# A hybrid decoder layer in split fp32: seven blocks through Strassen's products where five were, and the gates' silu in one ScalarE instruction

## The chip, the cores and the metric

The kernel runs as one program on one core of a Trainium2 chip. The metric is the device time of an execution in microseconds, the median of three runs. The engines are TensorE (PE; its weight loads are PEld), VectorE (DVE), ScalarE (ACT), GpSimd (POOL) and SyncE (SP), which issues most DMAs.

## What is computed

One layer with two token mixers on 256 tokens of width 2048, fp32, then a SwiGLU FFN:

```
u = rmsnorm(x)
[qkv_A | z_A | b_A | a_A | q_B | k_B | v_B | g_B | gate_A | gate_B] = u @ w_in
o_A = rmsnorm(gated_delta_rule(silu(conv(qkv_A)), ...)) * silu(z_A)
o_B = group_norm(retention(rotary(q_B), rotary(k_B), v_B))  * silu(g_B)
h   = x + (sigmoid(gate_A) * o_A + sigmoid(gate_B) * o_B) @ w_out
h   = h + (silu(rmsnorm(h) @ w_gate) * (rmsnorm(h) @ w_up)) @ w_down
out = rmsnorm(h)
```

There are 8 heads in each mixer, with values of width 256.

## The kernel before

Every large product is done in split precision: a weight tile `raw` (128 x 2048) comes by DMA, ScalarE rounds it to `hi` (line 169), VectorE makes `lo = raw - hi` (line 170), and TensorE multiplies the activations, split in the same way, with `hi` and `lo`. There are two `hi`, two `lo` and three `raw` buffers, so that the next tiles are split while TensorE works on one.

Work is a list of *units*, each with one weight tile. In the first phase four blocks of two heads follow each other. A block has 12 feature-major units (keys, queries, values for mixer A with the short convolution, and the rotary parts of mixer B; lines 239 and 244), and five token-major blocks of 512 columns, numbered i = 0 to 4: the values of mixer B, silu gate and sigmoid gate of mixer B, silu gate and sigmoid gate of mixer A.

A plain token-major block is four units of 24 products of 512 columns (lines 296, 297, 301). A block in `SBLK` goes through `strassen` instead: the 2 x 2 form with seven products, in eight units of 21 products of 256 columns (line 372). Its weights come as 512 KB pieces, VectorE first makes four more combinations of each (lines 187 to 189), and the sums of the activations that it needs (`ush`, `usl`) are made once, from the 14th unit on. Its results stay in four PSUM banks until a last copy (line 386) and four VectorE additions (lines 388 to 392) make the tile `Z`.

The eight units of a Strassen block are spread between the block's main units by `SPOS`: (7, 7) means from main unit 7 on, over 7 main units. A block that isn't in `SBLK` stands in the main list. `EARLY` says from which unit on the main products leave the four PSUM banks that Strassen's results need.

Gates are applied in `gate_evac`: ScalarE takes sigmoid of the scaled PSUM (line 881); for silu VectorE then multiplies by the scaled PSUM again (line 883); VectorE multiplies into the mixer's output (line 885), and after the last gate adds the two mixers (line 887). `merge` transposes the sum on TensorE (line 906) and splits it into the operand of the output projection (lines 914, 915). The second half of that operand shares memory with `ush`, so it can be written only after the last Strassen product: block 2's merge waits in a tile `wait` in the buffer of `Z` and is split by `split_rest` (lines 541, 542). Only for the last block the merge follows at once, and the 16 units of the output projection (`wo`) come next.

A scheduler reorders each engine's instructions in this list when the kernel is built; the resulting order is fixed. A second part of the list (the output projection and the FFN) is not touched.

Of the kernel before, what the change touches and what calls it, by code (L numbers as in the profile page):

```python
# [9 lines left out]
AF = mybir.ActivationFunctionType  # L10
ALU = mybir.AluOpType

P = 128
D = 2048
KT = D // P
S = 256
# [6 lines left out]

NWARM = 10
HOLD, SUMS_AT = 2, 14
EARLY = 28
Q2 = 2
SQ = 4
W_AT0, W_AT, W_TR0, W_TR = 6, 1, 5, 1
# [1 line left out]
SP_BEFORE, SP_AFTER = 2, 1  # L31


SBLK = [(), (2, 3), (2, 3), (3,)]
SPOS = [(), ((7, 7), (16, 8)), ((6, 9), (15, 9)), ((10, 14),)]
SIDE = [(b, i) for b in range(NBLK) for i in SBLK[b]]
MAIN = [(b, i) for b in range(NBLK) for i in range(5) if i not in SBLK[b]]

# [28 lines left out]
def kernel(  # L67
# [5 lines left out]
    V, A_, PE, G = nc.vector, nc.scalar, nc.tensor, nc.gpsimd  # L73
# [16 lines left out]
    def ps_turn(who, pools, name):  # L90
        turns_of[who] += 1
        tag, pool = pools[turns_of[who] % len(pools)]
        return pool.tile([P, 512], F32, tag=tag, name=name)
# [4 lines left out]
    def ps_mix(name):  # L98
        if first[0] and unit[0] < EARLY:
            return ps_turn("mix", [("mx", mx), ("pp", pp)], name)  # L100
        return ps_turn("mix", [("mx", mx), ("sp", sp)] if sums_away() else [("mx", mx)], name)

    def ps_unit(name):
        if not first[0]:
            return ps_turn("unit", [("pp", pp), ("mx", mx)], name)
        if unit[0] < EARLY:
            return ps_turn("unit", [("sp", sp)], name)
# [83 lines left out]
    def after(n, fn):  # L191

        events.setdefault(done[0] + n, []).append(fn)
# [88 lines left out]
    def flat(t):  # L282
        return t.rearrange("p a b -> p (a b)")
# [175 lines left out]
    mm = {}  # L459
# [8 lines left out]
    def t2(name):  # L468
        return mixp.tile([P, 512], F32, tag="t2", name=name, bufs=T2B)

    def mt(shape, tag, name, dt=F32):
        return mixp.tile(shape, dt, tag=tag, name=name)

    rstd_t = mixp.tile([P, NC], F32, name="rstd_t")
    rstd_b = mixp.tile([P, S], F32, name="rstd_b")
    Ei = mixp.tile([P, NBLK, 4, P], F32, name="Ei")
# [8 lines left out]
    def halves(t):  # L485
        return t.rearrange("p (a b) -> p a b", a=2)
# [39 lines left out]
    def new_parts(i):  # L526

        mm[i] = act.tile([P, KT // 2, 2, S], F32R, tag=f"a{2 + i}", name=f"m{i}")

    def merged_parts(b, j):  # L530
        k = 4 * (b % 2) + 2 * j
        return mm[b // 2][:, k:k + 2, 0], mm[b // 2][:, k:k + 2, 1]
# [28 lines left out]
    def block(b):  # L561
# [302 lines left out]
        def gate_evac(i, which, silu):  # L864
            def evac(pst):
                if which + "_done" not in T:
                    after(1, lambda: evac(pst))
                    return
                left[0] -= 1
                if left[0] == 0 and b == NBLK - 1:  # L870
                    with tc.high_priority(offset=100):
                        run(pst)
                else:
                    run(pst)

            def run(pst):
                o = T[which]
                for c in range(NC):
                    sg = halves(t2(f"gs_{b}_{i}_{c}"))
                    oc = halves(o[:, c])  # L880
                    A_.activation(sg, pst[c], AF.Sigmoid, scale=rstd_t[:, c:c + 1])
                    if silu:
                        V.scalar_tensor_tensor(out=sg, in0=pst[c], scalar=rstd_t[:, c:c + 1], in1=sg,
                                               op0=ALU.mult, op1=ALU.mult)
                    V.tensor_tensor(out=oc, in0=oc, in1=sg, op=ALU.mult)
                    if left[0] == 0:
                        mm["last"] = V.tensor_tensor(out=halves(T["oa"][:, c]), in0=halves(T["oa"][:, c]),
                                                     in1=halves(T["ob"][:, c]), op=ALU.add).ins
                if left[0] == 0:
                    if b == NBLK - 1:  # L890
                        merge(0)
                        merge(1)
                    else:
                        after(1, lambda: merge(0))
                        after(1, lambda: merge(1))
            return evac

        def merge(j):
            oa = T["oa"]
            if b == 0 and j == 0:  # L900
                new_parts(0)
            ps = ps_mix(f"pmt_{b}_{j}")
            for i in range(2):
                for c in range(NC):
                    f = (2 * j + i) * P
                    PE.transpose(out=ps[:, i * S + c * P:i * S + (c + 1) * P], in_=oa[:, c, f:f + P],
                                 identity=ident)
            if b // 2 not in mm:
                if j == 0:
                    mm["wait"] = flat(mt([P, 5, S], "Z", "wait"))  # L910
                A_.activation(mm["wait"][:, 512 * j:512 * j + 512], ps, AF.Copy)
                return
            hv, lv = merged_parts(b, j)
            A_.activation(hv, halves(ps), AF.Copy)
            V.tensor_tensor(out=lv, in0=halves(ps), in1=hv.bitcast(F32), op=ALU.subtract)
# [15 lines left out]
        for i, evac in enumerate(evacs):  # L931
            if i in SBLK[b]:
                sides.append(strassen(wsm[SIDE.index((b, i))], (uh, ul, LateSums(), usl), z_tiles, f"t{i}" + n,
# [15 lines left out]
    for b in range(NBLK):  # L949
        main, sides = block(b)  # L950
        for i, side in enumerate(sides):
            streams.append((len(mains) + SPOS[b][i][0], SPOS[b][i][1], side))
        mains += main
# [112 lines left out]
    with tc.tile_pool(name="ffn", bufs=1) as ffn:  # L1066
# [200 lines left out]
        with tc.manual_schedule(engines={nc.vector.engine}):  # L1267
# [4 lines left out]
            for c in range(NC):  # L1272
                for q in range(4):
                    ps = ps_sums(f"po_{c}_{q}")
                    for j in range(4):
# [3 lines left out]
                                    in1=wfs[:, 4 * q:4 * q + 4].unsqueeze(2).to_broadcast([P, 4, P]), op=ALU.mult)  # L1279
# [101 lines left out]
```

## Time and profile before

| | us |
|---|---|
| median of 3 runs | 1645.02 (1644.33 to 1645.72) |
| profiled execution | 1644.22 |
| its span | 1642.4 |
| TensorE busy | 1617.0 (98%) |
| VectorE busy | 1304.3 (79%) |
| ScalarE busy | 845.6 (51%) |
| GpSimd busy | 34.6 (2%) |

The times on the page are those of one execution under the profiler; the span goes from its first to its last recorded instruction. Busy shares are means over stages with different limits: what a stage waits for is read from stretches and from the engines in order of time. Matmuls are pipelined: the busy time of one (0.4 us for 512 columns) is longer than the distance to the next, so units are measured from start to start.

### The profile page before, as it was taken

Reading aid. Unit: us, or ns where it says so; the run is one execution under the profiler, and the core shown is the slowest. Engines: PE = TensorE matmul, PEld = TensorE weight load, DVE = VectorE, ACT = ScalarE, POOL = GpSimd, SP = SyncE. Lnnn points to the kernel's source line nnn. Section 1 sums busy time; section 2 is a strip of 40 time slices with the busy share of each in tenths; the row PEclk is TensorE's granted clock in tenths of the full one; section 3 lists DMA queues with packets and bytes.
Section 4 is the critical chain, followed back from the end, with each engine's and each line's share of the span. In section 5 each row is a group of like instructions: output and inputs, shape, how many; then the busy total and the mean of one; then the engine's idle time right before and its main releaser. Section 6 shows DMA issues by size and latency. Waiting matters only on the chain.

```text
span 1642.4 us, 24810 instructions
## 1 busy us (share of the span) xinstructions
PE 1617.0 (98%) x10202; PEld 1406.1 (86%) x10202; DVE 1304.3 (79%) x1680; ACT 845.6 (51%) x873; POOL 34.6 (2%) x64
## 2 busy tenths in 40 slices
PE   8999999999999999999999999999999999999998
PEld 6887888888888888888788888888888888888887
DVE  7797468887898878876776878889988899878764
ACT  5864455455554555445555654444554445545442
POOL 0000000000000000000000100000000000000000
PEclk8999999999999999999999999999999999999999
DMA  7454454555545565444674556556674566755751
GB/s 273 154 179 170 164 176 148 180 167 183 193 156 179 170 201 197 143 166 156 219 268 156 176 181 217 165 167 194 204 244 136 185 193 188 239 180 181 233 197 52
DMA packets 90450, 300.98 MB, mean 183 GB/s; under 512 B 6752, under 2 KB 11104, under 8 KB 74592
## 3 DMA queue, kind: packets, MB, share of 16 engines
q1 hardware_dynamic: 88896, 295.31, 53.8%
q10 hardware_dynamic: 1440, 4.08, 0.7%
q8 instruction: 80, 1.31, 0.3%
q14 instruction: 34, 0.28, 0.0%
HBM read 297.27 MB, written 2.10 MB: 182 GB/s over the span
## 4 chain that ended last, share of the span: by engine, by line
PE 91%; DVE 3%; DMA 1%; ACT 1%; issue 0%; POOL 0%; ACTq 0%; DVEq 0%
PE ps_wd L325 14%; PE pst_su L372 7%; PE ps_t L296 7%; PE ps_t L297 7%; PE ps_t L301 7%; PE ps_wu L325 7%; PE pst_t L372 6%; PE ps_wg L325 6%; PE pst_sg L372 6%; PE ps_r L239 4%; PE ps_wo L239 4%; PE ps_v L239 3%; PE ps_wo L244 2%; PE ps_r L244 2%; PE ps_v L244 1%; PE ps_q L239 1%
## 5 line engine op out<-in xcount | busy, mean ns | idle before, releaser
L169 ACT ACTIVATE hi_t<-raw_t 128x2048 fp32r<-128x2048 f32 (+1 forms) x100 | 183.1, 1831 | 220.8 <-PE ps_t L297 138.8
L170 DVE TENSOR_TENSOR lo_t<-raw_t,hi_t 128x2048 fp32r<-128x2048 f32 (+1 forms) x100 | 218.1, 2181 | 67.9 <-ACT hi_t L169 56.5
L296 PE MATMUL ps_t<-hi_t,u 128*128 128x512 f32 x480 | 192.0, 400 | 0.4 <-ACT vr L827 0.4
L297 PE MATMUL ps_t<-hi_t,u 128*128 128x512 f32 x480 | 188.3, 392 | 0.0
L325 PE MATMUL ps_wd<-hi_wd,f 128*128 128x512 f32 x704 | 170.8, 391 | 1.0 <-DVE f L1191 1.0
L325 PEld LDWEIGHTS ps_wd<-hi_wd,f 128*128 128x128 f32 x704 | 129.9, 188 | 27.4 <-DVE f L1191 1.2
L169 ACT ACTIVATE hi_sg<-raw_sg 128x1792 fp32r<-128x1792 f32 x48 | 81.6, 1702 | 118.7 <-DVE raw_sg L189 68.0
L169 ACT ACTIVATE hi_su<-raw_su 128x1792 fp32r<-128x1792 f32 x48 | 81.5, 1699 | 86.5 <-DVE raw_su L189 51.2
L170 DVE TENSOR_TENSOR lo_su<-raw_su,hi_su 128x1792 fp32r<-128x1792 f32 x48 | 97.0, 2022 | 35.0 <-ACT hi_su L169 19.7
L301 PE MATMUL ps_t<-lo_t,u 128*128 128x512 f32 x480 | 121.6, 392 | 0.0
L169 ACT ACTIVATE hi_wd<-raw_wd 128x2048 fp32r<-128x2048 f32 x44 | 84.3, 1915 | 70.2 <-PE ps_wd L325 27.8
L170 DVE TENSOR_TENSOR lo_wd<-raw_wd,hi_wd 128x2048 fp32r<-128x2048 f32 x44 | 100.6, 2286 | 19.8 <-ACT hi_wd L169 19.7
L170 DVE TENSOR_TENSOR lo_sg<-raw_sg,hi_sg 128x1792 fp32r<-128x1792 f32 x48 | 96.9, 2020 | 16.0 <-PE ps_wd L325 7.8
L296 PEld LDWEIGHTS ps_t<-hi_t,u 128*128 128x128 f32 x480 | 90.2, 188 | 18.7 <-ACT vr L827 0.6
L301 PEld LDWEIGHTS ps_t<-lo_t,u 128*128 128x128 f32 x480 | 89.7, 188 | 18.7
L297 PEld LDWEIGHTS ps_t<-hi_t,u 128*128 128x128 f32 x480 | 90.2, 188 | 17.7
L325 PE MATMUL ps_wd<-lo_wd,f 128*128 128x512 f32 x352 | 89.9, 396 | 3.6 <-DVE lo_wd L170 3.6
L325 PEld LDWEIGHTS ps_wd<-lo_wd,f 128*128 128x128 f32 x352 | 65.6, 190 | 17.2 <-DVE lo_wd L170 4.2
L325 PE MATMUL ps_wg<-hi_wg,h 128*128 128x512 f32 x320 | 78.9, 392 | 0.3 <-ACT hi_wg L169 0.3
L325 PE MATMUL ps_wu<-hi_wu,h 128*128 128x512 f32 x320 | 76.5, 390 | 0.0
L325 PEld LDWEIGHTS ps_wu<-hi_wu,h 128*128 128x128 f32 x320 | 59.2, 188 | 11.7
L325 PEld LDWEIGHTS ps_wg<-hi_wg,h 128*128 128x128 f32 x320 | 58.3, 188 | 11.6 <-ACT hi_wg L169 0.8
(333 smaller groups left out, 3358.5 us busy)
## 6 DMA issues: line engine op xcount, KB each, us to landing
raw_t<-in_wtm_dram SPq DMA_DIRECT2D x60, 1024.0 KB, 4.8
raw_wd<-in_wdown_dram SPq DMA_DIRECT2D x44, 1024.0 KB, 5.2
raw_sg<-in_wst_dram SPq DMA_DIRECT2D x48, 512.0 KB, 3.5
raw_su<-in_wst_dram SPq DMA_DIRECT2D x48, 512.0 KB, 3.6
raw_t<-in_wsm_dram SPq DMA_DIRECT2D x40, 512.0 KB, 3.5
raw_wg<-in_wgate_dram SPq DMA_DIRECT2D x20, 1024.0 KB, 5.1
raw_wu<-in_wup_dram SPq DMA_DIRECT2D x20, 1024.0 KB, 5.2
raw_v<-in_wqk_dram SPq DMA_DIRECT2D x16, 1024.0 KB, 4.8
```

The source lines that it names most:

```text
L169: ia = A_.activation(hi[:, r], w[:, r], AF.Copy)
L170: iv = V.tensor_tensor(out=lo[:, r], in0=w[:, r], in1=hi[:, r].bitcast(F32), op=ALU.subtract)
L239: PE.matmul(o[0], w, flat(a(k)), start=(k == 0), stop=(k == nk - 1), skip_group_check=True)
L244: PE.matmul(o[0][:, :S], lo[:, k * P:(k + 1) * P], a(k)[:, 0], start=False, stop=(k == nk - 1), skip_group_check=joined)
L296: PE.matmul(pst[c], uh[:, k, c * P:(c + 1) * P], w, start=(k == 0), stop=False)
L297: PE.matmul(pst[c], ul[:, k, c * P:(c + 1) * P], w, start=False, stop=False)
L301: PE.matmul(pst[c], uh[:, k, c * P:(c + 1) * P], lo[:, j * 512:(j + 1) * 512], start=False, stop=(k == KT - 1))
L325: PE.matmul(pst[c], u[:, k, c * P:(c + 1) * P], w[:, k], start=(start and k == 0 and q == 0), stop=(stop and k == 3))
L372: PE.matmul(T[bank][:, half * S:(half + 1) * S], op(j), w[:, slot * 256:(slot + 1) * 256], start=(j == 0 and w is hi and h and half == 0), ...
```

## The change

Two blocks more go through Strassen's products: i = 3 (mixer A's silu gate) in block 0, and i = 2 (mixer B's sigmoid gate) in block 3. Their plain units leave the main lists, and the side units are placed anew: in block 0 over nine main units from the 22nd on, so that they reach into block 1; in block 3 over main units 4 to 12 and 13 to 23, where 23 is the block's last main unit. `EARLY` goes from 28 to 20. `wait` moves from the buffer of `Z` to the first half of `Ei`, which only blocks 0 and 1 read. Silu is one ScalarE instruction.

```diff
-EARLY = 28
+EARLY = 20
...
-SBLK = [(), (2, 3), (2, 3), (3,)]
-SPOS = [(), ((7, 7), (16, 8)), ((6, 9), (15, 9)), ((10, 14),)]
+SBLK = [(3,), (2, 3), (2, 3), (2, 3)]
+SPOS = [((22, 9),), ((7, 7), (16, 8)), ((6, 9), (15, 9)), ((4, 9), (13, 11))]
...
-                    A_.activation(sg, pst[c], AF.Sigmoid, scale=rstd_t[:, c:c + 1])
-                    if silu:
-                        V.scalar_tensor_tensor(out=sg, in0=pst[c], scalar=rstd_t[:, c:c + 1], in1=sg,
-                                               op0=ALU.mult, op1=ALU.mult)
+                    A_.activation(sg, pst[c], AF.Silu if silu else AF.Sigmoid, scale=rstd_t[:, c:c + 1])
                     V.tensor_tensor(out=oc, in0=oc, in1=sg, op=ALU.mult)
...
-                    mm["wait"] = flat(mt([P, 5, S], "Z", "wait"))
+                    mm["wait"] = Ei[:, 0:2].rearrange("p a b c -> p (a b c)")
```

TensorE at the end of the first phase, before. `ps_t43` is the last plain block (i = 4 of block 3), `ps_wo1` and `ps_wo0` are the first blocks of the output projection, `m0` and `m1` its operand's halves, `pmt` the last merge's transposes.

```order
L301 MATMUL ps_t43_1_7489<-lo_t43_3_7545,u2_93 128x512 x4
L239 MATMUL ps_wo1_7701<-m0_2039,hi_wo1_7646 128x512 [waits Activation_49]
L239 MATMUL ps_wo1_7701<-m0_2039,hi_wo1_7646 128x512 x7
L239 MATMUL ps_wo1_7701<-m1_7462,hi_wo1_7646 128x512 x4
L906 MATMUL pmt_3_0_7604<-cs_74,oa_3_7121 128x128 [waits DVE_49]
L906 MATMUL pmt_3_1_7611<-cs_74,oa_3_7121 128x128
L239 MATMUL ps_wo0_7658<-m0_2039,hi_wo0_7640 128x512 x8
L239 MATMUL ps_wo0_7658<-m1_7462,hi_wo0_7640 128x512 x4
```

The same place in the changed kernel. `pst_t33` are the results of the Strassen block i = 3 of block 3.

```order
L372 MATMUL pst_t33_1_7183<-lo_t33_7_7771,ush_1103 128x256
L239 MATMUL ps_wo1_7942<-m0_2366,hi_wo1_7887 128x512 [waits Activation_49]
L239 MATMUL ps_wo1_7942<-m0_2366,hi_wo1_7887 128x512 x7
L239 MATMUL ps_wo1_7942<-m1_7825,hi_wo1_7887 128x512 [waits DVE_49]
L239 MATMUL ps_wo1_7942<-m1_7825,hi_wo1_7887 128x512
L239 MATMUL ps_wo1_7942<-m1_7825,hi_wo1_7887 128x512 [waits DVE_49]
L239 MATMUL ps_wo1_7942<-m1_7825,hi_wo1_7887 128x512
L903 MATMUL pmt_3_0_7845<-cs_74,oa_3_7464 128x128 [waits DVE_49,PE_49]
L903 MATMUL pmt_3_1_7852<-cs_74,oa_3_7464 128x128
L239 MATMUL ps_wo0_7899<-m0_2366,hi_wo0_7881 128x512 x8
L239 MATMUL ps_wo0_7899<-m1_7825,hi_wo0_7881 128x512 x4
```

A Strassen product is now the last of the phase, and the products with `m1` wait for VectorE.

ScalarE at that place, before. `hi_wo0` and `hi_wo1` are the splits of the first output weights, `gs_3_2` and `gs_3_3` the gates i = 3 and i = 4 of block 3.

```order
L169 ACTIVATE hi_t43_3_7544<-raw_t43_3_7514 128x2048 [waits DMAHW5_49,DVE_49,PE_49]
L881 ACTIVATE gs_3_2_0_7474<-Z_t33_7467,rstd_t_99 128x512 [waits DVE_49]
L881 ACTIVATE gs_3_2_1_7478<-Z_t33_7467,rstd_t_99 128x512
L169 ACTIVATE hi_wo0_7640<-raw_wo0_7638 128x2048 [waits DMAHW6_49,PE_49,Activation_49]
L169 ACTIVATE hi_wo1_7646<-raw_wo1_7644 128x2048 [waits DMAHW7_49,DVE_49,PE_49]
L881 ACTIVATE gs_3_3_0_7596<-ps_t43_0_7488,rstd_t_99 128x512 [waits DVE_49,PE_49]
L881 ACTIVATE gs_3_3_1_7600<-ps_t43_1_7489,rstd_t_99 128x512 [waits DVE_49,PE_49]
```

The same place in the changed kernel; `s1_t33` is the copy of line 386, `m1<-Ei` the split of block 2's merge.

```order
L169 ACTIVATE hi_wo0_7881<-raw_wo0_7879 128x2048 [waits DMAHW6_49,PE_49,Activation_49]
L881 ACT_TABLE_LOAD
L881 ACTIVATE gs_3_3_0_7798<-ps_t43_0_7581,rstd_t_99 128x512 [waits PE_49]
L881 ACTIVATE gs_3_3_1_7801<-ps_t43_1_7582,rstd_t_99 128x512 [waits PE_49]
L169 ACTIVATE hi_wo1_7887<-raw_wo1_7885 128x2048 [waits DMAHW7_49,DVE_49,PE_49]
L386 ACTIVATE s1_t33_7831<-pst_t33_2_7184 128x256 [waits PE_49,Pool_49]
L541 ACTIVATE m1_7825<-Ei_101 128x2x256 [waits PE_49]
L541 ACTIVATE m1_7825<-Ei_101 128x2x256
L881 ACT_TABLE_LOAD [waits DVE_49]
L881 ACTIVATE gs_3_2_0_7837<-Z_t33_7830,rstd_t_99 128x512 [waits Activation_49]
L881 ACTIVATE gs_3_2_1_7841<-Z_t33_7830,rstd_t_99 128x512 [waits Activation_49]
```

The gate i = 4 has come ahead of the second output weights' split, the gate i = 3 behind it, each with a table load; the second load stands behind a wait for VectorE.

VectorE there in the changed kernel, from the first addition of `Z` to the sum of the mixers:

```order
L388 TENSOR_TENSOR Z_t33_7830<-pst_t33_0_7182,s1_t33_7831 128x512
L542 TENSOR_TENSOR m1_7825<-Ei_101,m1_7825 128x2x256 x2
L389 TENSOR_TENSOR Z_t33_7830<-pst_t33_2_7184,Z_t33_7830 128x256
L390 TENSOR_TENSOR Z_t33_7830<-pst_t33_3_7185,Z_t33_7830 128x512
L392 TENSOR_TENSOR Z_t33_7830<-pst_t33_1_7183,Z_t33_7830 128x512
L882 TENSOR_TENSOR oa_3_7464<-oa_3_7464,gs_3_2_0_7837 128x512
L882 TENSOR_TENSOR oa_3_7464<-oa_3_7464,gs_3_2_1_7841 128x512
L884 TENSOR_TENSOR oa_3_7464<-oa_3_7464,ob_3_7324 128x512 x2
```

The same work before: the additions stood before the subtraction of the last plain unit, and that block's gate came last.

```order
L388 TENSOR_TENSOR Z_t33_7467<-pst_t33_0_6650,s1_t33_7468 128x512
L389 TENSOR_TENSOR Z_t33_7467<-pst_t33_2_6652,Z_t33_7467 128x256
L390 TENSOR_TENSOR Z_t33_7467<-pst_t33_3_6653,Z_t33_7467 128x512
L392 TENSOR_TENSOR Z_t33_7467<-pst_t33_1_6651,Z_t33_7467 128x512
L170 TENSOR_TENSOR lo_t43_3_7545<-raw_t43_3_7514,hi_t43_3_7544 128x2048
```

On VectorE the order now has four additions, two subtractions, two multiplies and two adds in one chain ahead of the merge.

## Rows read from the trace of the kernel before

**Rows 1.** The page, busy time of each engine over the span.
```profile
PE 1617.0 (98%) x10202; PEld 1406.1 (86%) x10202; DVE 1304.3 (79%) x1680; ACT 845.6 (51%) x873; POOL 34.6 (2%) x64
```

**Rows 2.** Stretches: us, busy us (instructions) by engine, granted clock, DMA share, GB/s.
```profile
242.00:270.00 28.00, 28.00 (x168) 24.86 (x167) 25.07 (x51) 15.76 (x36) 1.31 (x5) 1.00 0.36 117
270.00:320.00 50.00, 50.00 (x531) 44.99 (x530) 45.96 (x73) 26.39 (x27) 1.41 (x4) 1.00 0.51 169
418.00:520.00 102.00, 102.00 (x833) 90.77 (x832) 93.73 (x152) 55.84 (x77) 2.86 (x10) 1.00 0.50 168
700.00:810.00 110.00, 109.46 (x621) 92.82 (x620) 79.40 (x103) 54.39 (x51) 4.02 (x2) 1.00 0.52 179
```

**Rows 3.** TensorE in order: start us, us, line, instruction, count. Three units' first rows.
```profile
785.01 0.52 PE L372 MATMUL pst_t<-hi_t,u 128*128 128x256 f32 x3
...
787.51 0.40 PE L296 MATMUL ps_t<-hi_t,u 128*128 128x512 f32 x1
...
792.98 0.39 PE L296 MATMUL ps_t<-hi_t,u 128*128 128x512 f32 x1
```

**Rows 4.** Chain that ended last: the first key unit of blocks 2 and 3.
```profile
418.77 3.65 PE ps_k L239 x16
...
613.47 3.65 PE ps_k L239 x16
```

**Rows 5.** TensorE in order, end of the first phase; idle before, releaser.
```profile
807.49 1.98 PE L301 MATMUL ps_t<-lo_t,u 128*128 128x512 f32 x8
810.23 3.06 PE L239 MATMUL ps_wo<-m,hi_wo 128*128 128x512 f32 x12 [0.76 <-ACT gs L881]
813.12 0.38 PE L906 MATMUL pmt<-cs,oa 128*128 128x128 f32 x2
...
818.02 1.66 PE L239 MATMUL ps_wo<-m,hi_wo 128*128 128x512 f32 x6 [1.08 <-DVE m L915]
```

**Rows 6.** ScalarE in order, the same place.
```profile
788.69 0.37 ACT L386 ACTIVATE s_t<-pst_t 128x256 f32<-128x256 f32 x1
...
807.69 1.92 ACT L169 ACTIVATE hi_wo<-raw_wo 128x2048 fp32r<-128x2048 f32 x1 [3.47 <-PE ps_t L297]
809.51 1.24 ACT L881 ACTIVATE gs<-ps_t,rstd_t 128x512 f32<-128x512 f32 x2
...
825.92 5.52 ACT L169 ACTIVATE hi_wo<-raw_wo 128x2048 fp32r<-128x2048 f32 x3 [5.11 <-DMA raw_wo<-in_wout_dram]
```

**Rows 7.** VectorE in order, the same place.
```profile
795.53 0.69 DVE L388 TENSOR_TENSOR Z_t<-pst_t,s_t 128x512 f32<-128x512 f32 x1
...
797.44 0.69 DVE L392 TENSOR_TENSOR Z_t<-pst_t,Z_t 128x512 f32<-128x512 f32 x1
...
810.21 1.29 DVE L885 TENSOR_TENSOR oa<-oa,gs 128x512 f32<-128x512 f32 x2 [3.67 <-ACT gs L881]
811.42 1.29 DVE L887 TENSOR_TENSOR oa<-oa,ob 128x512 f32<-128x512 f32 x2
```

**Rows 8.** The gates' instructions: ns min/median/max, first and last start.
```profile
L883 DVE SCALAR_TENSOR_TENSOR gs<-ps_t,rstd_t,gs x10: 737/742/745, 151.3 to 755.9; 128x512 f32<-128x512 f32 x10
L881 ACT ACTIVATE gs<-Z_t,rstd_t x10: 707/709/725, 344.7 to 799.2; 128x512 f32<-128x512 f32 x10
...
L881 ACT ACT_TABLE_LOAD  x4: 1283/1283/1283, 149.0 to 753.1; - x4
```

**Rows 9.** The program's start: two stretches, and TensorE in order.
```profile
24.00:32.00 8.00, 4.97 (x38) 2.50 (x37) 8.00 (x10) 1.92 (x1) 0.27 (x1) 0.50 0.35 134
32.00:36.00 4.00, 4.00 (x26) 3.40 (x23) 2.33 (x3) 0.51 (x1) 2.46 (x2) 0.93 0.91 287
...
28.10 0.59 PE L995 MATMUL ss_n<-ones,sx 128*128 128x1 f32 x2 [3.02 <-DVE sx L991]
```

**Rows 10.** ScalarE in order, a table load between two stages of block 1.
```profile
343.38 1.28 ACT L881 ACT_TABLE_LOAD   x1
344.68 0.72 ACT L881 ACTIVATE gs<-Z_t,rstd_t 128x512 f32<-128x512 f32 x1
```

## The prediction

> **What bounds the kernel now.** I read the page's first part, then a table by stretch, then engines in order of time around the end of the first phase. TensorE is busy for 1617.0 of 1642.4 us [rows 1]; over the last 110 us of the first phase it is idle for 0.54 [rows 2]. So in the touched phase the path is TensorE's own stream of products: fewer products shorten the run by their full time, and every wait put into the stream lengthens it by its full time. VectorE is the second engine: 93.73 of 102 us while block 2 begins, with TensorE idle for nothing beside it [rows 2]. ScalarE at half load costs something only where TensorE waits for it.
>
> **The products.** One unit of a plain block (24 products of 512 columns) takes 792.98 - 787.51 = 5.47 us, a Strassen unit (21 of 256) 787.51 - 785.01 = 2.50 [rows 3]. Four plain units become eight Strassen units: 21.9 against 20.0, a gain of 1.9 per block, 3.8 for both blocks. Whole blocks say less: block 2 with two Strassen streams lasts 613.47 - 418.77 = 194.7, block 3 with one 809.47 - 613.47 = 196.0 (its end is 807.49 + 1.98) [rows 4, 5], 1.3 per stream, because each change between kinds of unit costs a little. I take the whole blocks, -2.6, and keep -3.8 as the other end. The weights stay 4 MB a block, in eight transfers of half the size on SP's queue, which keeps its order; I cost that at nothing, hidden by DMA at about half load [rows 2].
>
> **The silu.** 16 VectorE instructions of 0.74 go away [rows 8], 12 us in all. None lies on TensorE's path, so they are worth nothing directly; they make room for the subtractions of the new streams. In exchange, sigmoid and silu now need different tables: the order has 25 table loads where it had 19, 1.28 us each [rows 8]. Beside plain units that is hidden, since ScalarE is busy for 54 of 110 us [rows 2]; in one place it is not.
>
> **The end of the first phase** decides. Call T0 the end of the last plain product: 809.47 before [rows 5]. Before, the gate of that block was two ScalarE reads (1.24) [rows 6], two multiplies and two adds (1.29 each) [rows 7]; meanwhile TensorE did 24 products of the output projection that need nothing of it, and stood still for 0.76 and 1.08. It took up the products that need the last merge at 818.02, T0 + 8.55 [rows 5].
>
> Now a Strassen unit is the very last, so four additions, a gate, a table load and the earlier block pair's split follow T0 as well, in the order that the listings of the change show. Step by step, in us after T0:
> - ScalarE: the split of output weights 0 starts where the last split before T0 started (807.69, T0 - 1.78) and ends at 0.14 (1.92); load 1.28, 1.4; the sigmoid pair 1.24, 2.7; the split of output weights 1, 1.92, 4.6; the copy s1 0.37, about 4.9 [rows 6, 8]. TensorE finished its last Strassen product at 2.5 and cannot begin the output projection before 4.6: first pause 2.1.
> - VectorE: first addition 0.69, 5.6; the two subtractions of line 542 stand in between, 1.29 for a pair of 128x512 as at 811.42, 6.9; the other three additions 797.44 + 0.69 - 796.22 = 1.91, 8.8 [rows 7].
> - ScalarE: the second load stands behind a wait for the last addition, 1.28, 10.1; first silu 0.71, 10.8 [rows 8].
> - VectorE: two multiplies 1.29 and the first add 0.65, 12.7 [rows 7]. Only now can the first transposes run. TensorE did its 12 independent products by 7.5 (2.9 from 4.6, as 810.23 to 813.12) [rows 5]: second pause 5.2.
> - From the first transposes to the dependent products: 818.02 - 813.12 = 4.9 as before, 17.6 [rows 5].
>
> 17.6 less 8.55, less the 2.5 of the Strassen unit that lies in this stretch now, is +6.55. Bounds: if the ScalarE split of weights 1 and the copies overlap more, 5.5; if every hand-over costs another 0.1 to 0.15, 8.
>
> The wait for the load queues the merge's copies, the DMA issues for hT and the split of weights 2 behind it on ScalarE; they shift with the chain and cost nothing more. One thing behind it does: four products of output block 3 now stand before the low half of block 2. Their split began on ScalarE at 825.92, after a DMA wait, and ended at 827.84, 9.8 after the restart [rows 6]; TensorE is there after 8 + 16 products of 0.228 and 32 of 0.119 (the units' 5.47 / 24 and 2.50 / 21), 9.3. +0.5, between 0 and 1.5.
>
> **The clock.** At the program's start TensorE waited 3.02 us before 28.10, and the granted clock stood at 0.50 (1.2 GHz) from 24 to 32 and at 0.93 over 32 to 36, so it was back at 1.00 (2.4 GHz) near 32.6 [rows 9]: 4.5 us at half speed from 28.10, 2.2 lost. The second pause here is longer, and the work behind it (12 products, six transposes) stands in line before the restart, so I add +2.2. The ends are 0 (the clock does not fall) and about 3 (it falls in the first pause already).
>
> **VectorE in the new streams.** Block 0's stream ends in block 1, so its four additions, two multiplies, two adds and the merge's two subtractions move behind 242: 2.6 + 3 x 1.29 = 6.5 us [rows 7] onto 25.07 + 45.96 of 78 us [rows 2]: 77.5, full. I cost it at nothing, since block 2 has carried this very load, at 93.73 of 102, with TensorE never idle [rows 2]. If that cover is not enough, TensorE waits for low halves, up to about 4.
>
> **The sum.** -2.6 + 6.55 + 0.5 + 2.2 = +6.65. The profiled execution took 1644.22 us (span 1642.4 and 1.8 around it), so 1650.9; the median of the three runs is 0.8 above it: 1651.7.
>
> **A rule weighed.** Rows show a load that began at 343.38 and took 1.28 us, and the gate behind it beginning at 344.68, 0.02 us later [rows 10]. The Trainium skill (ScalarE: Activation LUTs, "What ACT_TABLE_LOAD costs") states about 1283 ns for the load, which the rows agree with, and a drain of about 1380 ns on top for every switch, which these rows do not show. By its 2.66 us a switch the two loads in the chain would make an estimated 2.8 us more, some 1654.5.
>
> **Rivals.**
> 1. The clock stays at 1.00, because the 12 products between the pauses are enough work: +4.45, 1649.5. For it: those 2.9 us of products; against: [rows 9].
> 2. VectorE becomes the bound, in block 1's beginning or where block 3's first stream now lies beside its convolution units: up to 4 more, 1655.7. For it: the 77.5 of 78; against: block 2.
> 3. Each load holds ScalarE for twice its row, as a drain behind it would: two on the chain, 2 x 1.28 more, 1654.3. Against: [rows 10].
> 4. Faster: the chain after T0 is hidden, because ScalarE has split weights 0 and 1 and done both loads (6.4 us in all) before T0. Then nothing is added at the end and the products' gain is left: 1641.2 to 1642.4. It decides as soon as the first transposes run by T0 + 6.2. Against it: the first split waits for the last plain unit's products, and the second load for the last addition, by the listing.
> 5. In between: half of the chain is hidden and the clock holds: +1 to +3, about 1647.
>
> **Chances.** Forecast 0.40, rival 1 0.25, rival 2 0.10, rival 3 0.04, rival 4 0.08, rival 5 0.13. About 0.2%, 3.3 us, can be told from no change. The forecast and rivals 1 to 3 lie above that: slower 0.78; rival 5 and a little of 1 and 4 within: 0.14; most of 4: faster 0.08. The forecast's own range, from its bounds, is 1647 to 1655.5; to leave out no more than 2 in 10 it reaches down over rival 5 and up over rival 2: 1644.5 to 1656.
>
> **What would show it.** The profile after: Strassen units at about 2.5 and blocks 0 and 3 each shorter by 1.3; no waits above 1 us in blocks 0 to 2; between the last Strassen product and the first merge transposes two pauses of TensorE, about 2 and 5, the second ended by VectorE's add; a granted clock near 0.5 for some 4 us behind it. It is wrong if that stretch takes under 12 us from the last plain product to the restart, or if new waits of several us stand in blocks 0 or 3 themselves.

## The result and the profile after

The changed kernel takes 1654.29 us (median of 4 runs, 1652.24 to 1655.33) against 1645.37 us of the kernel before on the same chip (4 runs): a ratio of 1.0053 with a 95% interval of 1.004 to 1.0065. Its profiled execution took 1653.26 us, its span 1651.5, 9.1 us more than the span before. Two runs of e8 below stand far above all others (3454.76 us, the profiled one, and 1764.16 us), and the comparison leaves them out.

The 9.1 us sit in one place. All products of the first phase end at 809.97 (the row at 809.33 below and its 0.64) against 809.47 before: +0.5. From there to the first product that needs the last merge pass 17.88 us against 8.55 before [rows 5]: +9.33. The rest of the program is 0.7 us shorter (1651.5 - 827.85 = 823.65 against 1642.4 - 818.02 = 824.38).

Even the +0.5 does not come from the blocks. The same products at the program's start, ahead of everything that the change touches, ran later in this execution (TensorE in order; the first two rows before, the last two after):

```profile
32.27 1.35 PE L244 MATMUL ps_q<-u,lo_q 128*128 128x256 f32 x8
42.28 3.82 PE L239 MATMUL ps_v<-u,hi_v 128*128 128x512 f32 x16
...
32.28 2.07 PE L244 MATMUL ps_q<-u,lo_q 128*128 128x256 f32 x8
43.01 3.82 PE L239 MATMUL ps_v<-u,hi_v 128*128 128x512 f32 x16
```

Up to 32.3 both are level. The granted clock, 0.50 over 28 to 32 in both, came back later in the changed kernel: over 33 to 34 it was 1.00 before and still 0.50 after. So 0.73 of the difference (43.01 against 42.28) is there before the changed code begins. In the profiles of this document (e8's apart) this product starts anywhere from 41.76 to 43.24. Below, the length of the first blocks is therefore counted from it.

TensorE of the changed kernel in order, as in [rows 5]: start, duration, line, instruction, count, and in brackets the idle time before it with what ended it.

```profile
805.49 1.98 PE L301 MATMUL ps_t<-lo_t,u 128*128 128x512 f32 x8
...
809.33 0.64 PE L372 MATMUL pst_t<-lo_t,ush 128*128 128x256 f32 x4
812.09 4.61 PE L239 MATMUL ps_wo<-m,hi_wo 128*128 128x512 f32 x12 [2.12 <-ACT hi_wo L169]
820.20 0.66 PE L903 MATMUL pmt<-cs,oa 128*128 128x128 f32 x2 [3.50 <-DVE oa L884]
820.51 5.47 PE L239 MATMUL ps_wo<-m,hi_wo 128*128 128x512 f32 x12
...
827.85 1.66 PE L239 MATMUL ps_wo<-m,hi_wo 128*128 128x512 f32 x6 [1.09 <-DVE m L912]
...
833.61 4.72 PE L239 MATMUL ps_wo<-m,hi_wo 128*128 128x512 f32 x20
```

T0, the end of the last plain product, is 807.47. There are two pauses, and both groups of twelve products take far longer than the 3.06 of [rows 5]. The granted clock goes with it. The same engine in stretches (columns as in [rows 2]; the clock is the third number from the right):

```profile
810.00:812.00 2.00, 0.00 (x0) 0.00 (x0) 1.88 (x3) 2.00 (x3) 0.00 (x0) 1.00 0.31 41
812.00:814.00 2.00, 1.91 (x5) 1.57 (x6) 1.66 (x3) 1.35 (x4) 0.00 (x0) 0.62 0.82 332
814.00:816.00 2.00, 2.00 (x6) 1.52 (x5) 1.93 (x4) 0.00 (x0) 0.00 (x0) 0.53 0.36 152
816.00:818.00 2.00, 0.70 (x3) 0.21 (x2) 0.02 (x1) 1.89 (x2) 0.00 (x0) 1.00 0.01 4
818.00:820.00 2.00, 0.00 (x0) 0.00 (x0) 1.85 (x4) 0.73 (x2) 0.00 (x0) 0.82 0.00 0
820.00:822.00 2.00, 1.80 (x6) 1.54 (x7) 2.00 (x3) 0.00 (x0) 0.00 (x0) 0.50 0.00 0
```

With TensorE idle the clock was still 1.00 over 810 to 812. It fell to 0.50 (1.2 GHz) when the first twelve had begun (0.96 over 812 to 812.5, 0.50 over the next half), was back at 1.00 (2.4 GHz) over 816 to 818, and fell again in the second pause; over 820 to 822, in the second twelve, it is 0.50.

ScalarE and VectorE over the same time, the rows that answer to [rows 6] and [rows 7]:

```profile
805.74 1.92 ACT L169 ACTIVATE hi_wo<-raw_wo 128x2048 fp32r<-128x2048 f32 x1 [1.99 <-issue]
807.68 1.28 ACT L881 ACT_TABLE_LOAD   x1
808.97 1.27 ACT L881 ACTIVATE gs<-ps_t,rstd_t 128x512 f32<-128x512 f32 x2
810.13 1.91 ACT L169 ACTIVATE hi_wo<-raw_wo 128x2048 fp32r<-128x2048 f32 x1
811.93 0.38 ACT L386 ACTIVATE s_t<-pst_t 128x256 f32<-128x256 f32 x1
...
816.10 1.28 ACT L881 ACT_TABLE_LOAD   x1 [2.75 <-DVE Z_t L392]
817.39 1.33 ACT L881 ACTIVATE gs<-Z_t,rstd_t 128x512 f32<-128x512 f32 x2
```

```profile
815.33 0.69 DVE L392 TENSOR_TENSOR Z_t<-pst_t,Z_t 128x512 f32<-128x512 f32 x1
818.15 1.30 DVE L882 TENSOR_TENSOR oa<-oa,gs 128x512 f32<-128x512 f32 x2 [2.13 <-ACT gs L881]
819.37 1.29 DVE L884 TENSOR_TENSOR oa<-oa,ob 128x512 f32<-128x512 f32 x2
```

The chain reads downwards, from engine to engine: split, load, sigmoid, split, copy, four additions, load, silu, multiplies, adds, then the transposes at 820.20. The load at 816.10 stands behind a wait for the last addition, so nothing hides it.

The start of block 3 (the chain that ended last, as in [rows 4]):

```profile
614.51 5.69 PE ps_k L239 x25
```

Block 3 lasts 809.97 - 614.51 = 195.46 (196.0 before), 0.54 less. From the product at the program's start to block 3 it takes 614.51 - 43.01 = 571.50, against 613.47 - 42.28 = 571.19 before: 0.31 more, so the first block's stream has not shortened what lies ahead of block 3. One new wait is there, in block 1 (TensorE in order):

```profile
274.00 1.16 PE L764 MATMUL pq<-qT,kT 128*128 128x128 f32 x8 [1.23 <-ACT jn_q L573]
```

VectorE is close to its limit, but hardly ever the bound (stretches of [rows 2], first engine column after the two of TensorE): 27.69 of 28 us with TensorE idle for nothing, then 45.90 of 50 with the wait just shown. In block 3 TensorE waits for it once, 0.44 us for a low half at 709.06 (line 301 for line 170).

```profile
242.00:270.00 28.00, 28.00 (x172) 25.13 (x171) 27.69 (x52) 17.66 (x31) 1.16 (x3) 1.00 0.51 169
270.00:320.00 50.00, 48.77 (x516) 43.31 (x515) 45.90 (x80) 24.60 (x35) 1.50 (x5) 1.00 0.46 152
...
700.00:810.00 110.00, 109.53 (x714) 93.46 (x712) 84.90 (x122) 56.84 (x52) 2.21 (x3) 1.00 0.53 177
```

### The profile page after: what moved, and what is told of

It is laid out like the page before. It is cut to its first block, busy times and chain, and to the rows that moved or that the text cites. A ratio compares the mean times of both kernels' runs of the same rounds, so it can differ in the third digit from the quotient of the medians.

```text
span 1651.5 us, 25199 instructions
## 1 busy us (share of the span) xinstructions
PE 1618.4 (98%) x10346; PEld 1413.4 (86%) x10346; DVE 1330.8 (81%) x1728; ACT 866.6 (52%) x889; POOL 32.9 (2%) x64
## 4 chain that ended last, share of the span: by engine, by line
PE 88%; DVE 5%; ACT 2%; issue 1%; DMA 1%; POOL 0%; ACTq 0%; DVEq 0%
PE ps_wd L325 13%; PE pst_t L372 8%; PE pst_su L372 7%; PE ps_wu L325 7%; PE ps_wg L325 7%; PE ps_t L296 6%; PE ps_t L301 6%; PE ps_t L297 6%; PE pst_sg L372 5%; PE ps_wo L239 4%; PE ps_r L239 3%; PE ps_v L239 3%; PE ps_wo L244 2%; PE ps_r L244 2%; PE ps_v L244 1%; PE ps_q L239 1%
## 5 line engine op out<-in xcount | busy, mean ns | idle before, releaser
L169 ACT ACTIVATE hi_t<-raw_t 128x2048 fp32r<-128x2048 f32 (+1 forms) x108 | 195.0, 1806 | 226.0 <-PE ps_t L297 108.0
L170 DVE TENSOR_TENSOR lo_t<-raw_t,hi_t 128x2048 fp32r<-128x2048 f32 (+1 forms) x108 | 232.2, 2150 | 70.1 <-ACT hi_t L169 61.1
L296 PE MATMUL ps_t<-hi_t,u 128*128 128x512 f32 x416 | 164.5, 395 | 0.4 <-ACT vr L827 0.4
L297 PE MATMUL ps_t<-hi_t,u 128*128 128x512 f32 x416 | 163.3, 393 | 0.0
L170 DVE TENSOR_TENSOR lo_wd<-raw_wd,hi_wd 128x2048 fp32r<-128x2048 f32 x44 | 100.5, 2285 | 19.8 <-ACT hi_wd L169 19.7
L301 PE MATMUL ps_t<-lo_t,u 128*128 128x512 f32 x416 | 106.4, 394 | 0.4 <-DVE lo_t L170 0.4
L301 PEld LDWEIGHTS ps_t<-lo_t,u 128*128 128x128 f32 x416 | 77.4, 188 | 16.9 <-DVE lo_t L170 0.9
L296 PEld LDWEIGHTS ps_t<-hi_t,u 128*128 128x128 f32 x416 | 78.2, 188 | 15.9 <-ACT vr L827 0.6
L297 PEld LDWEIGHTS ps_t<-hi_t,u 128*128 128x128 f32 x416 | 78.2, 188 | 15.0
L239 PE MATMUL ps_wo<-m,hi_wo 128*128 128x512 f32 x256 | 66.1, 412 | 3.2 <-ACT hi_wo L169 2.1
```

Of the source, the lines that this page charges most:

```text
L169: ia = A_.activation(hi[:, r], w[:, r], AF.Copy)
L170: iv = V.tensor_tensor(out=lo[:, r], in0=w[:, r], in1=hi[:, r].bitcast(F32), op=ALU.subtract)
L239: PE.matmul(o[0], w, flat(a(k)), start=(k == 0), stop=(k == nk - 1), skip_group_check=True)
L296: PE.matmul(pst[c], uh[:, k, c * P:(c + 1) * P], w, start=(k == 0), stop=False)
L297: PE.matmul(pst[c], ul[:, k, c * P:(c + 1) * P], w, start=False, stop=False)
L301: PE.matmul(pst[c], uh[:, k, c * P:(c + 1) * P], lo[:, j * 512:(j + 1) * 512], start=False, stop=(k == KT - 1))
```

## The experiments

Ratios are to the kernel before on the same chip, with their 95% intervals; T0 is each kernel's own end of its last plain product, "restart" the first product that needs the last merge (before: T0 + 8.55). The first four take the change apart.

**e1: the phase ends in a plain block again.**

```
-SPOS = [... ((4, 9), (13, 11))]
+SPOS = [... ((4, 9), (13, 7))]
```

> The changed kernel, with the last Strassen stream of block 3 over 7 main units instead of 11, so that four plain units stand behind its last product. Theory A (the exposed end of the phase: pauses of TensorE of 2.1 and 3.5 us and the half clock behind them cost 9.3 us): the pauses above 1.5 us and the half clock go, only a table load of 1.3 us stays in front of the last gate; 8 us less than the changed kernel, 1646 to 1647. Theory B (the end is only a part; the streams in blocks 0 and 3 load VectorE and ScalarE so much that TensorE waits elsewhere): at most 4 us less, 1650 or more, with waits in the blocks.

1648.81 us, ratio 1.0022 [1.0013, 1.003]: between the two theories. About 5 us of the loss go with the order at the end, but one pause is left, and it is long (TensorE in order):

```profile
807.97 1.98 PE L301 MATMUL ps_t<-lo_t,u 128*128 128x512 f32 x8
813.98 4.61 PE L239 MATMUL ps_wo<-m,hi_wo 128*128 128x512 f32 x12 [4.03 <-ACT gs L881]
```

What ScalarE did there, the load in front of the last gate:

```profile
811.94 1.28 ACT L881 ACT_TABLE_LOAD   x1 [1.80 <-DVE oa L882]
```

And on VectorE the work that this multiply of line 882 stood behind:

```profile
809.57 1.67 DVE L751 SCALAR_TENSOR_TENSOR oa<-oa,fp,gws 128x256 f32<-128x256 f32 x4
```

The gate waits for a VectorE multiply, that one for the scaling of line 751, which ends the delta rule of block 3. Before, that scaling began at 784.50, 25 us ahead of T0; here at 809.57, with T0 at 809.95. The delta rule moves on one step per *plain* unit (`done[0]` does not count Strassen units), and block 3 now has 24 of them, not 28. The changed kernel has it at 806.80, hidden there by the longer chain behind.

**e2: the old gates, with everything else changed.**

```
-A_.activation(sg, pst[c], AF.Silu if silu else AF.Sigmoid, ...)
+A_.activation(sg, pst[c], AF.Sigmoid, ...)
+if silu: V.scalar_tensor_tensor(out=sg, in0=pst[c], ..., in1=sg, ...)
```

> The changed kernel, with silu again as ScalarE's sigmoid and a VectorE multiply; seven Strassen blocks in the same places. Theory A: both table loads leave the chain behind the last plain unit, two VectorE multiplies (1.5 us) come into it; the first pause shrinks to about 1.3 us, the transposes come 0.5 us earlier, the second pause and the half clock stay: 1653.5 to 1654. Theory C (the table loads of the silu are what costs): 2.6 us or more less, 1651.5 or below.

1656.2 us, 1.0058 [1.0045, 1.0071]: theory C is out: no table load is left in the chain behind T0, and the restart is still at T0 + 19.8. Without the first load the first pause is 1.16 us, and the twelve products behind it take 3.34 us, nearly the full clock; the second pause grows to 5.21, and the next twelve take 5.47:

```profile
812.93 3.34 PE L239 MATMUL ps_wo<-m,hi_wo 128*128 128x512 f32 x12 [1.16 <-ACT hi_wo L169]
821.48 0.66 PE L906 MATMUL pmt<-cs,oa 128*128 128x128 f32 x2 [5.21 <-DVE oa L887]
821.80 5.47 PE L239 MATMUL ps_wo<-m,hi_wo 128*128 128x512 f32 x12
```

Theory A has the end of the phase right (transposes at T0 + 12.2), but its time is 2 us too low. In block 1 TensorE waits 2.38 us for the merge's subtraction on VectorE (line 915), and the clock falls behind that wait (0.60 over 274 to 276, 0.55 over 276 to 278).

**e3: the first block's stream alone** (with the silu).

```
-SBLK[3] = (2, 3);  SPOS[3] = ((4, 9), (13, 11))
+SBLK[3] = (3,);    SPOS[3] = ((10, 14),)
```

> The changed kernel, with block 3 as before the change (one Strassen stream, four plain units behind it); block 0's stream and the silu stay. Theory A: end of the phase as before but for one table load of 1.3 us; block 0 gains 1.3 from its products and loses 1.2 in the one wait seen in block 1 (TensorE for the squares of block 1's queries): 1646.5. Theory B: 1649 or more.

1647.77 us, 1.0009 [0.9999, 1.0019]: no change that can be told, nearer theory A. The wait at pq is there (1.2 us); block 3 starts at 614.23 against 613.47 [rows 4], of which 0.73 is there at the program's start (43.01 against 42.28); restart T0 + 9.9.

**e4: the silu alone** (the edit is against the kernel before).

```
-A_.activation(sg, pst[c], AF.Sigmoid, ...)
-if silu: V.scalar_tensor_tensor(out=sg, in0=pst[c], ..., in1=sg, ...)
+A_.activation(sg, pst[c], AF.Silu if silu else AF.Sigmoid, ...)
```

> The kernel before, with silu in one ScalarE instruction and nothing else. Theory A: VectorE's 12 us are off the path and bring nothing; the one table load in front of the last gate delays the last merge by up to 1.3 us: 1645.5 to 1646.7. Theory D (VectorE's relief is worth something to TensorE): below 1644.

1646.07 us, 1.0000 [0.9991, 1.0009], theory A. The load in front of the last gate adds 1.4 us (a pause of 2.19 instead of 0.76); behind the restart the profile is 1.2 shorter, in a part that no edit touches (the last section says what differs there). Behind that pause the twelve products keep the full clock:

```profile
811.78 3.02 PE L239 MATMUL ps_wo<-m,hi_wo 128*128 128x512 f32 x12 [2.19 <-ACT gs L881]
```

**e5: the clock by itself.** Work is added, none is taken away.

```
 begin()
+if not first[0] and unit[0] == 2:
+    for q in range(24):
+        PE.matmul(o[0], uh[:, q % KT, 0:P], flat(u2[:, q % KT]), start=True, stop=True, ...)
```

> The changed kernel with 24 more products of 128x512 (their result is overwritten, nothing waits for them) in front of the twelve ps_wo products behind the last Strassen unit. In the changed kernel TensorE pauses there twice, 2.12 and 3.50 us, and the twelve products behind each pause take 4.61 and 5.27 us where twelve take about 2.9 at the full clock. Theory A, the granted clock fell because of the pauses: 24 x 0.24 = 5.8 us of filler fill the first pause and push the first twelve to about 815.8 to 818.7, the second pause shrinks to 1 to 2 us, the clock stays at 1.00 in 810 to 826, the second twelve take 2.9 instead of 5.3, and the restart of the dependent products comes 2 to 2.8 us earlier although work was added: 1651.5 to 1652.3. Theory B, those products are slow for another reason (VectorE and ScalarE reading the same banks, or operands that come late): they stay at 4.6 and 5.3 us, nothing is gained and the filler may push the transposes: 1654 to 1657.

1652.43 us, 1.0038 [1.0026, 1.005]; theory A. The clock shows 1.00 from 806 to 836, and TensorE in order:

```profile
803.85 1.98 PE L305 MATMUL ps_t<-lo_t,u 128*128 128x512 f32 x8
...
808.17 5.64 PE L251 MATMUL ps_wo<-u 128*128 128x512 f32 x24
813.64 2.88 PE L239 MATMUL ps_wo<-m,hi_wo 128*128 128x512 f32 x12
818.57 0.41 PE L907 MATMUL pmt<-cs,oa 128*128 128x128 f32 x2 [2.04 <-DVE oa L888]
818.73 3.01 PE L239 MATMUL ps_wo<-m,hi_wo 128*128 128x512 f32 x12
...
823.48 1.66 PE L239 MATMUL ps_wo<-m,hi_wo 128*128 128x512 f32 x6 [1.09 <-DVE m L916]
```

The transposes stand at T0 + 12.74 as in the changed kernel (T0 is 805.83), the twelve behind them take 3.01 instead of 5.47, and the restart comes at T0 + 17.65 instead of 20.38. So 2.73 us of the loss are the clock, 24 added products notwithstanding. (The intervals of the two ratios overlap; it is the rows that settle it.)

**e6: both groups of twelve in front of the transposes.** In the changed kernel one group waits for a PSUM bank of the other pool.

```
 if not first[0]:
-    return ps_turn("unit", [("pp", pp), ("mx", mx)], name)
+    return ps_turn("unit", [("pp", pp)] if unit[0] < 3 else [("pp", pp), ("mx", mx)], name)
```

> The changed kernel, with the PSUM tiles of the first two output units both from the pool of the token-major products, so that both groups of twelve ready products stand in front of the first transposes; before, one group of twelve stood behind them. Theory A, the group behind the transposes lies on the path to the restart: both groups run from 810 to about 816, one pause of 4 to 4.5 us before the transposes at T0 + 12.7 (T0 = 807.5), and behind these only six transposes and the split: restart at about T0 + 15.5 to 17 instead of 20.4; 1650 to 1651.5 when the clock that falls in the longer pause takes 1 to 2 us back behind it. Theory B, the path is set by the clock and the longer pause costs what the order gains: 1653.5 to 1655.

1652.08 us, 1.0038 [1.0025, 1.0051], between the theories. The restart comes at 822.85, T0 + 16.0 (T0 is 806.82), as theory A has it, 4.4 us earlier; but the one long pause leaves the clock low behind the restart, where it takes some 2 us back (2.93 instead of 1.66 for the same six products):

```profile
819.54 2.06 PE L903 MATMUL pmt<-cs,oa 128*128 128x128 f32 x8 [4.16 <-DVE oa L884]
822.85 2.93 PE L239 MATMUL ps_wo<-m,hi_wo 128*128 128x512 f32 x6 [1.26 <-DVE m L912]
```

**e7: e1 with the delta rule of block 3 two steps earlier.**

```
-for _ in range(PAUSE_M):                       yield
+for _ in range(PAUSE_M if b < 3 else 1):       yield
-for _ in range(PAUSE_P if lv == 1 else 1):     yield
+for _ in range(PAUSE_P if lv == 1 and b < 3 else 1): yield
```

> The kernel of the first experiment (the second stream of the last block of heads stops four plain units earlier, so that a plain block ends the phase), with the delta rule's chain of the last block of heads advanced by two steps (one pause fewer at two places). Theory A, that kernel paused 4.03 us because the chain, which moves on once per plain unit and has 24 of them instead of 28, came out at 806: with two steps fewer the square roots and the scaling of oa are over before the phase ends, the gate waits for nothing but its products and the table load, the pause falls to about 2.2 us as in the kernels with five streams, restart at T0 + 10: 1645.5 to 1646.5. Theory B, the pause came from the table load and the queue of ScalarE: it stays near 4 us, 1648 to 1649.5.

1645.57 us, 0.9996 [0.9987, 1.0004]; theory A. The scaling stands at 796.93, 12 us ahead of T0 (808.75), the pause is that of e4, and e1's loss is gone:

```profile
810.93 4.62 PE L239 MATMUL ps_wo<-m,hi_wo 128*128 128x512 f32 x12 [2.19 <-ACT gs L881]
```

Here the clock fell behind a pause of 2.19 us, in e4 it did not behind one of the same length: restart T0 + 11.5, against T0 + 9.95. Inside the block the late chain had cost too: from the start of block 3 (613.98 in e1, 613.80 in e7) to T0 pass 195.97 in e1 and 194.95 in e7. A wait of TensorE for VectorE's low half, 0.7 in e1 and absent in e7, is the larger part of that.

**e8: e7 with the old gates and e6's banks.**

> Seven streams as in the kernel of the experiment before this, with the gates as in the kernel before (sigmoid and a multiply on VectorE, so no table load in front of the last gate), and both groups of ready output products in front of the transposes. Theory A, the streams do gain (about 0.5 us in the last block of heads, up to 1.3 in the first less a wait of 1.2) once the end of the phase is as short as in the kernel before: 1643 to 1645. Theory B, seven streams gain nothing because the sums of Strassen's units meet new waits: 1645 to 1647.

1647.09 us (median of ten), 1.0005 [0.9996, 1.0014]: theory A is out, and the time lies at the upper end of theory B. No profile of these ten is there, so where the time goes stays open.

**e9: e7 with the old gates** (e8 without the banks).

> The kernel with the early chain and the plain block last (seven streams), with the gates as in the kernel before: sigmoid on ScalarE and a multiply on VectorE, so no table load in front of the last gate. Theory A, what is left of the loss at the end of the phase is that load: the pause in front of the first twelve ps_wo products falls from 2.19 to about 0.8 us, the granted clock stays at 1.00 there, and the restart comes T0 + 8.6 as in the kernel before instead of T0 + 11.5: 1642.5 to 1644.5, below the kernel before by the gain of the streams. Theory B, the multiplies on VectorE and their waits give it back in the first phase and in the FFN part: 1645 to 1647.

1645.85 us, 1.0001 [0.9993, 1.001]: theory B for the time, though A's mechanism is there. The pause is 0.76, the clock holds, restart T0 + 8.55. But the wait in block 1 has doubled, now for the merge's subtraction on VectorE, which has the gates' multiplies to do as well:

```profile
274.74 0.66 PE L570 MATMUL pss_q<-cs,qT 128*128 128x128 f32 x4 [2.53 <-DVE m L915]
...
811.95 3.06 PE L239 MATMUL ps_wo<-m,hi_wo 128*128 128x512 f32 x12 [0.76 <-ACT gs L881]
```

**e10: the second stream of the last block alone** (with the silu): `SBLK[0] = ()`, `EARLY = 28`.

> The changed kernel without the stream in the first block of heads: six streams, two of them in the last block, which ends in a Strassen unit. Theory A, the two parts add up: the whole change measured a ratio of 1.0053 and the first block's stream alone 1.0009, so this one gives about 1.004 to 1.005, 1652.5 to 1654.5, with the restart of the dependent products about T0 + 20 as in the changed kernel. Theory B, the loss needs both streams (the chain of the last block is pushed by the first): 1.002 or less, 1650 or below.

1652.73 us, 1.0044 [1.003, 1.0058]; theory A. With e3's 1.0009 the parts add up to the whole change's 1.0053. The pauses are 2.12 and 3.79 us.

**e11: silu in blocks 0 to 2, sigmoid and multiply in block 3, otherwise e7.**

```
+whole = silu and b < NBLK - 1
-A_.activation(sg, pst[c], AF.Silu if silu else AF.Sigmoid, ...)
+A_.activation(sg, pst[c], AF.Silu if whole else AF.Sigmoid, ...)
+if silu and not whole: V.scalar_tensor_tensor(...)
```

> Seven streams, the early chain, the plain block last; the gates by ScalarE's silu in the first three blocks of heads and by sigmoid and VectorE's multiply in the last block alone. Theory A, the two sides of the gates are priced apart: without a load in front of the last gate the restart comes at T0 + 8.6 to 9 (11.5 with silu everywhere), and without VectorE's multiplies in front of the first merge the wait in the second block of heads stays at 1.23 us (2.53 us with sigmoid everywhere): 1642.5 to 1644.5, some 1.5 to 3 us below the kernel before. Theory B, the rest of the program gives it back or the differences of single profiles were scatter: 1645 to 1646.5.

1643.79 us, 0.9989 [0.998, 0.9997], theory A: the only one of the twelve versions whose interval lies below 1, just so, by 1.7 us (1645.53 on the same chip). The wait in block 1 is 1.23 us, as forecast. TensorE at the end of the phase (T0 is 808.82, restart T0 + 8.55):

```profile
809.58 3.06 PE L239 MATMUL ps_wo<-m,hi_wo 128*128 128x512 f32 x12 [0.77 <-ACT gs L882]
...
817.37 1.66 PE L239 MATMUL ps_wo<-m,hi_wo 128*128 128x512 f32 x6 [1.08 <-DVE m L916]
```

The rows show 1.06 us of the gain, in block 3 (808.82 - 613.88 = 194.94 against 196.0). The profiled execution itself is not shorter than the one before (span 1642.9 against 1642.4), because the clock fell once more in the FFN, which costs 1.7 us (last section).

**e12: e11 with pss_q and pq of block 1 one unit later**: `W_AT + (b == 1)`.

> The same, with the scores of the delta rule in the second block of heads (pss_q and pq) one unit later, behind one more plain unit and not behind the transposes of the first merge, whose PSUM bank they take. Theory A, the wait of 1.23 us there is one for that bank and ends: block 2 starts about 1.2 us earlier against the kernel beside it, 1641.5 to 1643.5. Theory B, the wait moves to the next product that needs the same bank: no difference to the kernel beside it within 0.5 us.

1647.09 us, 1.0008 [0.9999, 1.0017]: worse than e11; theory B in kind, but not "no difference". The wait at pq is gone, and a product behind it waits in its place, for VectorE's reading of pq. Behind that wait the granted clock fell (stretches as above), which did not happen in e11:

```profile
282.68 0.45 PE L648 MATMUL pM<-Pc,MTc 32*32 32x32 f32 x32 [1.43 <-DVE at L769]
...
284.00:286.00 2.00, 2.00 (x14) 2.00 (x13) 2.00 (x4) 0.00 (x0) 0.00 (x0) 0.64 0.02 6
286.00:288.00 2.00, 2.00 (x30) 1.71 (x30) 2.00 (x7) 1.84 (x3) 0.00 (x0) 0.51 0.59 184
```

Counted from the product at the program's start, block 3 begins 2.9 us later than in e11 (616.24 - 42.06 against 613.88 - 42.57). The clock makes 1.7 of that. The rest are waits of 1.43, 0.31 and 0.67 in block 1, where e11 has the one of 1.23.

## Why the prediction came out as it did

The direction, the place and the mechanism of the loss were right; the gain that should have stood against it was not there. Term by term:

- **The chain after T0 held to within 0.3 us at every step.** Forecast in us after T0, then measured (T0 = 807.47): first output product 4.6, 4.62; last addition over 8.8, 8.55; second load over 10.1, 9.91; first transposes 12.7, 12.73. Restart without the clock's part 17.6; e5, which held the clock, has it at 17.65. The step "+6.55" was right. It came from durations of single rows, walked from engine to engine in the listed order.
- **The clock was sized a little low.** +2.2 was taken for a fall in the second pause; e5 prices that fall at 2.73, all of it behind the transposes. The fall behind the first pause, for which the bound of 3 stood, cost nothing: the transposes are at T0 + 12.73 with it and at T0 + 12.74 in e5 without it. It only made the second pause 3.50 and not 5.2, because the twelve products ahead of it took 4.61 and filled it. Rival 1, that the clock stays, is out.
- **The step that failed is the products' -2.6**, with the waits in the new streams put at nothing. Measured, they gained 0.23: 0.54 in block 3, less 0.31 lost ahead of it. In block 0 the stream's products gained about 0.9, and the wait of 1.23 at pq took it back. Seven kernels with silu and this stream have that wait (the changed one, e1, e3, e5, e6, e7, e11), and none without the stream has it: from the product at the program's start to block 3 pass 571.22 to 571.50 us in the seven, 571.19, 571.10 and 571.11 in the kernel before, e4 and e10. In block 3 the products gained 1.0, of which the wait of 0.44 for a low half took back nearly half; e10, without that wait, gained 1.02 (809.33 - 614.35 = 194.98 against 196.0), e7 1.05. So each stream's products are worth some 1 us, not 1.3, and the waits, 1.67 in all, took back most of it. One of the prediction's own signs, no wait above 1 us in blocks 0 to 2, failed here. The forecast asked whether VectorE had room. What came in block 1 was a wait for one short answer, of ScalarE (jn_q) or VectorE (e2, e9, e12), in a stretch where TensorE had nothing else in line. pq reads only queries and keys, so it is probably a PSUM bank that it waits for; no run isolates that. Busy shares do not show such a wait.
- **wo3's +0.5 was 0.** The twenty products at 833.61 show no wait. The split that they were to wait for began on ScalarE at 833.92, 6.1 us after the restart, where it had been 7.9 before [rows 6].
- **VectorE at 0** was right but for the 0.44, and **rival 2**, with up to 4 us, is out. **Rival 3**, a load at twice its row: out. The rows at 816.10 and 817.39 leave 0.01 us between load and gate; the drain that the Trainium skill (ScalarE: Activation LUTs, "What ACT_TABLE_LOAD costs") puts on each switch is not seen.
- **Rivals 4 and 5**, the chain hidden or half hidden: out, by the two pauses.

The forecast fell short by 2.6 us, or 2.4 between the profiled executions: 2.4 from the products, 0.6 from chain and clock, 0.7 from the start of the program, less 0.5 for wo3 and 0.7 for the rest of the program. That the start and the rest cancel is luck: both lie in code that the change does not touch. One sum in the forecast does not come out: its named bounds add to at most -2.6 + 8 + 1.5 + 3 = +9.9, that is 1654.9, and not 1655.5.

## What to carry to other kernels

Where a phase ends in products that depend on a chain of small steps, the order of the last units is worth more than the products saved: walk the chain from the last independent product, row by row. Look also at what advances per unit: with units of another kind, chains counted in the old kind come out later. A pause that lowers the clock is paid again in the products behind it (1.6 and 2.4 us for twelve here), so where they are on the path the price of a wait is more than its length. Before a gain or loss of 1 or 2 us is read from one profile, compare the granted clock in the parts that the edit does not touch.

## What the runs showed of the chip

The same pause of TensorE lowered the clock in one kernel and not in another. The pause of TensorE at the end of the phase, and what the twelve products of 512 columns behind it took:

| kernel | pause, us | twelve products, us |
|---|---|---|
| before, e9, e11, e12 | 0.76, 0.76, 0.77, 0.76 | 3.06 each |
| e2 | 1.16 | 3.34 |
| e5 (behind the transposes) | 2.04 | 3.01 |
| e10, after | 2.12, 2.12 | 4.32, 4.61 |
| e3, e4 | 2.19, 2.19 | 3.02, 3.02 |
| e7 | 2.19 | 4.62 |
| after (behind the transposes) | 3.50 | 5.47 |
| e10 (behind the transposes) | 3.79 | 4.53 |
| e1 | 4.03 | 4.61 |
| e2 (behind the transposes) | 5.21 | 5.47 |

After the pauses of 0.76 to 1.16 us the products kept the full clock or nearly so, after those of 3.5 us and more they did not; around 2.1 us both occurred, and no run here tells why.

It happens without any change of the code, too. The FFN, which no edit touches, has a pause of 2.17 to 2.63 us in each of the thirteen profiles (e8's apart), ahead of eight products with a low half. Here it is in e3 and in e7:

```profile
1287.93 2.11 PE L325 MATMUL ps_wd<-lo_wd,f 128*128 128x512 f32 x8 [2.62 <-DVE lo_wd L170]
...
1287.76 2.88 PE L325 MATMUL ps_wd<-lo_wd,f 128*128 128x512 f32 x8 [2.62 <-DVE lo_wd L170]
```

In e3 the clock stayed at 1.00, in e7 it fell (0.50 over 1290 to 1292). It fell behind this pause in nine of the thirteen, and behind a second one of 2.20 us some 75 us later in five; each fall cost 1.7 us. e3 and e4 have none, the kernel before and the changed one have one, e7 and e11 two. So the restart of e7 at T0 + 11.5 and that of e4 at T0 + 9.95 may differ by this alone.

Sigmoid and silu did not share a table: the changed kernel loads 25 times, the kernel before 19.
